# Hybrid decoder layer on one core: rope queries behind each latent tile, gate tiles beside the sums of x, and paced row loads in the down projection

## Chip, cores and metric

One core of a Trainium2 chip runs the whole layer as one program. The metric is device microseconds (us) of an execution. Matrix products run on TensorE (PE in the profile), everything elementwise on VectorE (DVE), ScalarE (ACT) and GpSimd (POOL); DMAs are issued from the queues of SyncE (SP), ACT and POOL.

## The reference, cut to what matters

```python
proj = h @ w_in[i]                      # 1024 x 1024 times 1024 x 5792
qkv, z, b_raw, a_raw, cq, ckv, kr, gate_dn, gate_mla = jnp.split(proj, SPLIT_IDX, axis=-1)
beta = jax.nn.sigmoid(b_raw)
g = -jnp.exp(dn_a_log[i]) * jax.nn.softplus(a_raw + dn_dt_bias[i])     # decays of the gated DeltaNet
...
c_q = rms_norm(cq, q_norm_w[i])                                        # query latent, 384 wide
q_nope, q_rope = jnp.split(jnp.einsum('bsc,chd->bshd', c_q, w_uq[i]), [MLA_NOPE], axis=-1)
q_rope = apply_rope(q_rope, cos, sin)                                  # 8 heads x 64
c_kv = rms_norm(ckv, kv_norm_w[i]); k_rope = apply_rope(kr, cos, sin)  # key latent, 256 wide
...
h = layer_norm(ALPHA * h + mixed @ w_o[i], ln1_g[i], ln1_b[i])
gt, up = jnp.split(h @ w_ffn_in[i], 2, axis=-1)
ffn = (jax.nn.silu(gt) * up) @ w_ffn_out[i]                            # down projection, 2816 x 1024
```

The sequence has 1024 tokens, in 8 tiles of 128. Everything is float32.

## The kernel before

Every float32 operand of a product is split into two parts, `hi` (a cast on ACT, L63) and `lo` (the remainder, on DVE, L64), and a product is three matmuls: hi·hi, hi·lo and lo·hi. A planner inside the language orders the instructions of each engine: it takes what is ready by its own timing model, earlier lines first, so work that is written later can run earlier. On the chip each engine then runs its list in that order.

**The first stage** (L129 to L397) makes everything of `proj` that is not in pairs:
- L182 to L206: the first three of the 24 *gate tiles* (`z` and the two gates; 48 matmuls each on two of the PSUM banks A to D), while x arrives. The third one's weights lie in memory of `cqT`.
- L265 to L289: the *latent tiles*. For `ckv` (336 columns with the key rope and the decays' inputs) and then for `cq` (384 columns), each of 8 token tiles takes 24 matmuls into a PSUM tile `s`, a sum of squares on ACT, a scale on DVE and POOL, the product with the norm weight on DVE (L285), 2 or 3 transposes on PE (L288) and a split into `ckvT` or `cqT`. The weights `wA` have 8 buffers, so those of `cq` follow when the last tile of `ckv` gives them back.
- L302 to L351: rope of the keys and the decays (some 35 small operations on DVE and ACT).
- L353 to L395: gate tiles 3 to 6 (L164 to L176), and for each token tile the *rope queries*: 9 matmuls (L379), six DVE operations (L294 to L299), a split, 8 transposes (L393), two copies on ACT (L394) into `qt` (two buffers), and a store to `qr_d` issued from POOL (L395). The latents are spilled to DRAM (`lat_d`) in six large stores from POOL.
- L420 to L440: the sums of x (`T1` to `T4`) that the seven-product scheme of the next stage needs, with their splits. Gate tile 7 is written between them (L435). Then `pair` (L458, products at L480) runs, whose matmuls may not start before the last rope transpose (L616).

**The last stage** (L1357 to L1498) is the down projection in seven products (n = 1, 2, 7, 5, 6, 3, 4), each of 11 steps (k) with 12 matmuls per step (L1433). A step loads an activation form (`x_form`, L1372: two `xs` buffers with a split into three `xh` buffers for n = 1 and 2; straight into `xh`, 2 x 256 KB, for n = 3, 5, 6, 7) and takes a weight form (`w_form`, L1387) from rows of `w_ffn_out`, four quarters of 11 rows of 256 KB. Quarter (0, 0) is loaded in `open_down`; `load_rows` brings the others ahead of the product that first uses them:

```python
        if n == 2:
            load_rows((0, 1))
        elif n == 7:
            load_rows((1, 0))
        elif n == 5:
            load_rows((1, 1))
```

The planner is free to issue all of these loads, all on SP's queue, as soon as their memory is free.

Of the kernel before, what the change touches and what calls it, by code (L numbers as in the profile page):

```python
# [17 lines left out]
P = 128  # L18
# [18 lines left out]
def tile_hybrid_block(ctx: ExitStack, tc: tile.TileContext, A: dict):  # L37
# [143 lines left out]
    pp = pool(p1, "p1")  # L181
    p1w = ExitStack()  # L182
    pw1 = pool(p1w, "p1w")
    fw = [[[half_w(i) for i in range(2)] for _ in range(2)] for _ in range(2)]
    fps = [[bank(0), bank(1)], [bank(2), bank(3)], [s_tile(), s_tile()]]
    for k in range(KT):
# [7 lines left out]
        if k == 0:  # L194
            fv = [cqT[i][:, 0].rearrange("p (k a) -> p k a", k=KT) for i in range(2)]
            fw.append([[v[:, q * 4:q * 4 + 4] for v in fv] for q in range(2)])
# [68 lines left out]
    for off, wd, c0, n, dst in ((0, 336, CQ, 2, ckvT), (336, 384, 0, 3, cqT)):  # L265
        if off:
            wA = lat_w(off, wd)
        nl_ = n * P
        for t in range(NT):
            ts = slice(t * P, (t + 1) * P)  # L270
            ps = s_tile()
            for k in range(KT):
                for j, (a, b) in enumerate(HL):
                    nc.tensor.matmul(ps[:, 0:wd], xT[a][k][t // 4][:, t % 4 * P:(t % 4 + 1) * P], wA[k][b][:, 0:wd], start=(k == 0 and j == 0),
                                     stop=(k == KT - 1 and j == 2))
            if off == 0:
                nc.scalar.copy(kr_raw[:, t], ps[:, 256:320])
                nc.scalar.copy(ba[:, t], ps[:, 320:336])
            mr = pp.tile([P, 2], F32, name="mr", bufs=3)
            ms, rs = mr[:, 0:1], mr[:, 1:2]  # L280
            cn = pw1.tile([P, CQ], F32, name="cn", bufs=3)[:, 0:nl_]
            nc.scalar.activation(cn, ps[:, 0:nl_], AF.Square, accum_out=ms)
            nc.vector.tensor_scalar(ms, ms, 1.0 / nl_, 1e-6, op0=ALU.mult, op1=ALU.add)
            nc.gpsimd.tensor_tensor(rs, ms, nhalf[:, 0:1], ALU.pow)
            nc.vector.scalar_tensor_tensor(cn, ps[:, 0:nl_], rs, wn[:, c0:c0 + nl_], op0=ALU.mult, op1=ALU.mult)  # L285
            tp = s_tile("t")[:, 0:nl_].rearrange("p (n a) -> p n a", n=n)
            for j in range(n):
                nc.tensor.transpose(tp[:, j], cn[:, j * P:(j + 1) * P], ident)  # L288
            split(tp, dst[0][:, :, ts], dst[1][:, :, ts])  # L289

    p1w.close()
# [9 lines left out]
    kr2 = pp.tile([P, NT, 2, RD], F32, name="kr2")  # L301
    rtmp = pp.tile([P, NT, 32], F32, name="rtmp")  # L302
    rope(kr2[:, :, 0, 0:32], kr2[:, :, 0, 32:64], kr_raw[:, :, 0:32], kr_raw[:, :, 32:64], cos, sin, rtmp)
    nc.vector.tensor_copy(kr2[:, :, 1], kr2[:, :, 0])
    for hf in range(2):
        tp = s_tile("t").rearrange("p (t a) -> p t a", t=4)
        for t in range(4):
            nc.tensor.transpose(tp[:, t], kr2[:, hf * 4 + t].rearrange("p a b -> p (a b)"), ident)
        split(tp, *[k.rearrange("p (t a) -> p t a", t=NT)[:, hf * 4:hf * 4 + 4] for k in krT])

    for i in range(2):
        nc.gpsimd.dma_start(out=lat_d["ckv"][i], in_=ckvT[i])

    e1 = pp.tile([P, NT, H], F32, name="e1")
    nc.scalar.activation(e1, ba[:, :, 0:8], AF.Exp, scale=-1.0)
    nc.vector.tensor_scalar(e1, e1, 1.0, None, op0=ALU.add)
    nc.vector.reciprocal(beta, e1)
    xa = pp.tile([P, NT, H], F32, name="xa")
    nc.vector.tensor_tensor(xa, ba[:, :, 8:16], alog[:, 1].unsqueeze(1).broadcast_to([P, NT, H]), ALU.add)
    na = pp.tile([P, NT, H], F32, name="na")  # L320
    nc.vector.scalar_tensor_tensor(na, xa, -1.0, xa, op0=ALU.mult, op1=ALU.min)
    y = pp.tile([P, NT, H], F32, name="y")
    nc.scalar.activation(y, na, AF.Exp)
    den = pp.tile([P, NT, H], F32, name="den")
    nc.vector.tensor_scalar(den, y, 2.0, None, op0=ALU.add)
    nc.vector.reciprocal(den, den)
    sa = pp.tile([P, NT, H], F32, name="sa")
    nc.vector.tensor_tensor(sa, y, den, ALU.mult)
    s2 = pp.tile([P, NT, H], F32, name="s2")
    nc.vector.tensor_tensor(s2, sa, sa, ALU.mult)  # L330
    acc = pp.tile([P, NT, H], F32, name="acc")
    nc.vector.tensor_scalar(acc, s2, 2.0 / 17, 2.0 / 15, op0=ALU.mult, op1=ALU.add)
    for n in (13, 11, 9, 7, 5, 3, 1):
        nc.vector.tensor_tensor(acc, acc, s2, ALU.mult)
        nc.vector.tensor_scalar(acc, acc, 2.0 / n, None, op0=ALU.add)
    nc.vector.tensor_tensor(acc, acc, sa, ALU.mult)
    nc.vector.scalar_tensor_tensor(acc, xa, 0.0, acc, op0=ALU.max, op1=ALU.add)
    nea = row[:, 24:32]
    nc.scalar.activation(nea, alog[:, 0], AF.Exp)
    g = pp.tile([P, NT, H], F32, name="g")  # L340
    nc.vector.scalar_tensor_tensor(g, acc, -1.0, nea.unsqueeze(1).broadcast_to([P, NT, H]), op0=ALU.mult, op1=ALU.mult)
    split(g, g_hl[:, 0], g_hl[:, 1])
    gc = s_tile()[:, 0:P].rearrange("p (a t h) -> p a t h", a=2, t=NT)
    nc.tensor.matmul(gc[:, 0], m_le, g, start=True, stop=True)
    nc.tensor.matmul(gc[:, 1], ones, g, start=True, stop=True)
    nc.scalar.activation(eg, gc[:, 0], AF.Exp)
    nc.scalar.activation(egl, gc[:, 1], AF.Exp)
    gcs = pp.tile([P, NT, H], F32, name="gcs")
    nc.vector.tensor_copy(gcs, gc[:, 0])
    nc.vector.tensor_tensor(gcs, gc[:, 1], gcs, ALU.subtract)  # L350
    nc.scalar.activation(egd, gcs, AF.Exp)  # L351

    gate_tile(3)  # L353
    gate_tile(4)
    w5 = load_w(A["w_main"][24 + 5])


    pb_s = ExitStack()
    pb = pool(pb_s, "p1b")
    wq = [pb.tile([P, 3, 512], F32R, name=f"wq{i}") for i in range(2)]  # L360
    for k in range(3):
        st = wpool.tile([P, 512], F32, name="wst", bufs=2)
        nc.sync.dma_start(out=st, in_=A["w_uq_rope"][:, k])
        split(st, wq[0][:, k], wq[1][:, k])
    SPILL = {2: [("kr", krT, 0), ("kr", krT, 1)], 3: [("cq", cqT, 0)], 4: [("cq", cqT, 1)]}
    for t in range(NT):
        if t == 0:
            gate_tile(5, w5)
        if t == 3:
            gate_tile(6)  # L370
        for nm, v, i in SPILL.get(t, ()):
            nc.gpsimd.dma_start(out=lat_d[nm][i], in_=v[i].unsqueeze(1) if nm == "kr" else v[i])
        with tc.high_priority():
            ts = slice(t * P, (t + 1) * P)
            ps = s_tile()
            n = 0
            for k in range(3):
                for a, b in ((0, 0), (0, 1), (1, 0)):
                    nc.tensor.matmul(ps, cqT[a][:, k, ts], wq[b][:, k], start=n == 0, stop=n == 8)  # L379
                    n += 1  # L380
            pv = ps.rearrange("p (h r) -> p h r", h=H)
            qro = pb.tile([P, H, RD], F32, name="qro", bufs=2)
            qtmp = pb.tile([P, H, 32], F32, name="qtmp", bufs=1)
            cb = trigq[:, 0, t].unsqueeze(1).broadcast_to([P, H, 32])
            sb = trigq[:, 1, t].unsqueeze(1).broadcast_to([P, H, 32])
            rope(qro[:, :, 0:32], qro[:, :, 32:64], pv[:, :, 0:32], pv[:, :, 32:64], cb, sb, qtmp)
            stk = pb.tile([P, H, 2, RD], F32R, name="stk", bufs=2)
            split(qro, stk[:, :, 0], stk[:, :, 1])
            qt = pb.tile([P, H, P], F32R, name="qt", bufs=2)
            for hf in range(2):  # L390
                tp = s_tile("t").rearrange("p (h a) -> p h a", h=4)
                for h in range(4):
                    p1b_end = nc.tensor.transpose(tp[:, h], stk[:, hf * 4 + h].bitcast(F32).rearrange("p a b -> p (a b)"), ident)  # L393
                nc.scalar.copy(qt[:, hf * 4:hf * 4 + 4], tp)  # L394
            nc.gpsimd.dma_start(out=qr_d[:, :, ts].rearrange("h p n -> p h n"), in_=qt)  # L395
# [1170 lines left out]
```

## Time and profile before

| | us |
|---|---|
| median of 3 runs | 2138.59 (2135.35 to 2140.73) |
| the profiled execution's own time | 2146.9 |
| its span | 2145.1 |
| PE busy | 2051.5 (96%) |
| DVE / ACT / POOL busy | 1388.8 / 945.8 / 651.2 |
| mean granted clock of TensorE | 0.982 of full |

The busy share of PE counts a matmul as busy for longer when the granted clock is lower. So a stretch has to be read by its number of matmuls and its granted clock, not by its busy share alone. A row of the views by stretch gives, for each engine, the busy us and the number of instructions, then the clock, the busy share of the DMA engines and GB/s.

### The profile page before, as it was taken

The page shows a single profiled execution, that of the slowest core. Times are in us where ns is not written, and L with a number is a line of the kernel's source. Part 1 is how long each engine was busy: PE and PEld are TensorE (multiplying, and loading weights), DVE is VectorE, ACT ScalarE, POOL GpSimd, SP SyncE. Part 2 cuts the span into 40 slices and gives each one's busy share as a digit, 9 for nine tenths or more (in the row PEclk, how much of TensorE's full clock was granted, in tenths as well). Part 3 has the DMA queues.
Part 4 walks back from the last instruction along what each step waited for, and adds up shares of the span by engine and source line. Part 5 has one row for each costly group of instructions (what it writes and reads, how often), then busy time and mean ns, then how long its engine had stood idle before and what let it go on. Part 6 is the DMA issues. An engine that isn't in the chain of part 4 may idle for free.

```text
span 2145.1 us, 29573 instructions
## 1 busy us (share of the span) xinstructions
PE 2051.5 (96%) x10450; PEld 1718.9 (80%) x10450; DVE 1388.8 (65%) x2151; ACT 945.8 (44%) x1936; POOL 651.2 (30%) x569
## 2 busy tenths in 40 slices
PE   8998899999999999998999999999999999998998
PEld 6987578787878888786887788899888888886876
DVE  4434988797955655443645356487878788864476
ACT  5333556776675555444433223243333333333233
POOL 0112443444342899840210000100111121111842
PEclk9999999999999999998999999999999999999999
DMA  6236345556566321137986666025434344376562
GB/s 221 73 131 169 103 171 185 172 186 212 198 212 248 102 75 59 58 109 211 293 246 208 209 221 237 22 87 178 148 112 144 128 143 134 114 246 246 192 230 108
DMA packets 225892, 350.86 MB, mean 164 GB/s; under 512 B 43792, under 2 KB 118352, under 8 KB 224464
## 3 DMA queue, kind: packets, MB, share of 16 engines
q1 hardware_dynamic: 208400, 318.67, 44.8%
q0 software_dynamic: 12736, 22.02, 3.5%
q10 hardware_dynamic: 4608, 8.27, 1.1%
q8 instruction: 83, 1.36, 0.3%
q14 instruction: 65, 0.53, 0.1%
HBM read 228.01 MB, written 120.88 MB: 163 GB/s over the span
## 4 chain that ended last, share of the span: by engine, by line
PE 62%; DMA 11%; DVE 7%; ACT 6%; issue 2%; POOL 1%; SPq 0%; POOLq 0%; ACTq 0%; DVEq 0%
PE f L1433 6%; PE A L1242 5%; PE s L1199 4%; PE f L1115 4%; PE f L717 4%; PE B L1242 3%; PE D L1242 3%; PE E L1242 3%; PE C L1242 3%; PE F L1242 3%; PE o L741 2%; PE C L480 2%; PE D L480 2%; PE B L480 2%; PE p L689 2%
## 5 line engine op out<-in xcount | busy, mean ns | idle before, releaser
L1433 PE MATMUL f<-wh,xh 128*128 128x512 f32 x792 | 186.6, 395 | 10.7 <-ACT xh L63 9.0
L1433 PEld LDWEIGHTS f<-wh,xh 128*128 128x128 f32 x792 | 150.0, 190 | 46.5 <-ACT xh L63 11.1
L63 ACT CAST w<-S 128x512 fp32r<-128x512 f32 x168 | 103.5, 618 | 137.0 <-PE D L1242 42.9
L1341 POOL TENSOR_TENSOR T<-act 128x512 f32<-128x512 f32 x22 | 32.2, 1463 | 402.0 <-DVE act L1326 231.0
L64 DVE TENSOR_TENSOR w<-S,w 128x512 fp32r<-128x512 f32 x168 | 131.5, 783 | 25.5 <-ACT w L63 21.2
L1242 PE MATMUL A<-m,w 128*128 128x512 f32 x504 | 121.2, 389 | 0.0
L876 PE MATMUL y<-om,w 128*128 128x512 f32 x384 | 103.5, 414 | 8.5 <-ACT w L63 3.5
L1242 PEld LDWEIGHTS A<-m,w 128*128 128x128 f32 x504 | 94.5, 188 | 19.6
L805 POOL TENSOR_TENSOR nl<-nl,itmp 128x486 f32<-128x486 f32 (+44 forms) x106 | 105.5, 1012 | 1.4
L803 POOL TENSOR_TENSOR itmp<-nl 128x486 f32<-128x486 f32 (+44 forms) x106 | 95.0, 914 | 17.3 <-DMA nl<-n_d 12.8
L1088 POOL TENSOR_TENSOR lrs<-sm,nhalf 128x1 f32<-128x1 f32 x16 | 23.2, 1455 | 234.9 <-issue 140.1
L876 PEld LDWEIGHTS y<-om,w 128*128 128x128 f32 x384 | 71.5, 195 | 26.5 <-ACT om L63 4.7
L64 DVE TENSOR_TENSOR w<-wst,w 128x512 fp32r<-128x512 f32 (+1 forms) x54 | 51.7, 957 | 61.8 <-ACT w L63 61.8
L1115 PE MATMUL f<-wo,m 128*128 128x512 f32 x384 | 91.0, 392 | 0.6 <-DVE acc L1079 0.6
L1115 PEld LDWEIGHTS f<-wo,m 128*128 128x128 f32 x384 | 71.4, 188 | 15.5 <-DVE acc L1079 1.1
L63 ACT CAST w<-wst 128x512 fp32r<-128x512 f32 (+1 forms) x54 | 43.3, 808 | 91.8 <-DMA wst<-in_w_br_mla_dram 39.9
L64 DVE TENSOR_TENSOR pt<-t,pt 128x512 fp32r<-128x512 f32 (+1 forms) x96 | 52.2, 554 | 46.5 <-ACT pt L63 45.6
L741 PE MATMUL o<-pt,vv 128*128 128x512 f32 (+3 forms) x288 | 78.2, 374 | 3.5 <-ACT pt L63 1.4
L528 DVE SCALAR_TENSOR_TENSOR c<-zo,cw,c 128x1023 f32<-128x1023 f32 (+2 forms) x48 | 70.4, 1467 | 14.0 <-ACT c L526 13.8
L721 DVE TENSOR_REDUCE row<-f 128x1 f32<-128x128 f32 (+3 forms) x64 | 48.3, 755 | 42.1 <-PE f L719 41.5
L717 PE MATMUL f<-c,qn 128*128 128x512 f32 (+3 forms) x288 | 68.9, 357 | 1.8 <-ACT pr L723 1.8
L1199 PE MATMUL s<-r,m 128*128 128x256 f32 x576 | 69.7, 283 | 0.0
(479 smaller groups left out, 5388.1 us busy)
## 6 DMA issues: line engine op xcount, KB each, us to landing
acc<-in_w_ffn_in_dram SPq DMA_DIRECT2D x44, 512.0 KB, 4.0
xs_d<-xo SPq DMA_DIRECT2D x88, 256.0 KB, 2.5
xh<-xs_d SPq DMA_DIRECT2D x88, 256.0 KB, 2.8
wst<-in_w_main_dram SPq DMA_DIRECT2D x25, 512.0 KB, 4.7
a<-in_w_ffn_out_dram SPq DMA_DIRECT2D x44, 256.0 KB, 5.2
raw<-in_w_main_dram SPq DMA_DIRECT2D x20, 512.0 KB, 4.4
xs<-xf_d SPq DMA_DIRECT2D x33, 256.0 KB, 3.4
an_d<-c SPq DMA_DIRECT2D x16, 512.0 KB, 6.9
```

The source lines that it names most:

```text
L63: nc.scalar.copy(hi, src)
L64: nc.vector.tensor_tensor(lo, src, hi.bitcast(F32), ALU.subtract)
L480: nc.tensor.matmul(bk, w[a][:, k], x[b][k], start=(k == 0 and j == 0), stop=(k == 3 and j == 2))
L717: nc.tensor.matmul(ps[:, c * 512:c * 512 + w], l[:, qs], r[c][:, 0:w], start=n == 0, stop=(n == 4 and c != gq))
L741: nc.tensor.matmul(po[:, i0 * P:512], vv[kt][a][:, hh * P:(hh + 1) * P], hl[b][:, 0:w], start=(kt == 0 and j == 0), stop=(kt == last and j ...
L803: nc.gpsimd.tensor_tensor(tv, nl[:, k0:kn_, k:k + 1].broadcast_to([P, kn_ - k0, w]), nl[:, k:k + 1, k + 1:64].broadcast_to([P, kn_ - k0, w ...
L805: nc.gpsimd.tensor_tensor(nl[:, k0:kn_, k + 1:64], nl[:, k0:kn_, k + 1:64], tv, ALU.subtract)
L876: nc.tensor.matmul(ps, w[a][:, k], od[b][:, k, ns] if dn else om[k][b], start=(k == 0 and j == 0), stop=(k == KT - 1 and j == 2))
L1115: nc.tensor.matmul(ps[:, ns], mT[a][kh, t // 4][:, k % 4, t % 4 * P:(t % 4 + 1) * P], wo[k][b][:, ns], start=(k == 0 and j == 0), stop=(k ...
L1199: nc.tensor.matmul(ps, mT[a][k // 4, t // 4][:, k % 4, tq], wg[k][b], start=(k == 0 and j == 0), stop=(k == KT - 1 and j == 2))
L1242: nc.tensor.matmul(bank, w[a][:, k], x[b][:, k], start=(k == 0 and j == 0), stop=(k == 3 and j == 2))
L1433: nc.tensor.matmul(bk, x[a][:, t * P:(t + 1) * P], w[b], start=(k == 0 and j == 0), stop=(k == HH - 1 and j == 2))
```

## The change

It does four things.
1. The rope queries of tile t are written right behind the latent tile t of `cq` and take it from a two-buffer tile, on banks A to D; their weights are loaded and split ahead. `cqT`, `ckvT` and `krT` are gone: each latent piece is stored to DRAM at once, two stores per tile, issued from ACT. The `qr_d` store moves from POOL to SP.
2. The rope of the keys and the decays become a generator, `side`, of which one piece follows each rope tile.
3. Gate tiles 3 to 7 are written beside the sums of x: tile 3 ahead of the loop, one more in each of its four turns.
4. In the down projection one row is loaded per step, one product earlier than before, and each row and each load of `acc` is issued on SP only behind the newest activation load.

```diff
+    def latent(t, off, wd, c0, n, wA):
...
+        out = [latp.tile([P, n, P], F32R, name=f"l{n}{i}", bufs=2) for i in range(2)]
+        split(tp, *out)
+        for i in range(2):
+            nc.scalar.dma_start(out=lat_d["ckv" if off == 0 else "cq"][i][:, :, ts], in_=out[i].bitcast(F32))
+        return out
+
+    for t in range(NT):
+        latent(t, 0, 336, CQ, 2, wA)
+    wA = lat_w(336, 384)
+    wq = [wq_tile(i) for i in range(2)]
+    for k in range(3):
+        st = wpool.tile([P, 512], F32, name="wst", bufs=2)
+        nc.sync.dma_start(out=st, in_=A["w_uq_rope"][:, k])
+        split(st, wq[0][:, k], wq[1][:, k])
...
-    gate_tile(3)
-    gate_tile(4)
-    w5 = load_w(A["w_main"][24 + 5])
...
+    def rope_q(t, cq):
+        ts = slice(t * P, (t + 1) * P)
+        ps = bank(t % 2)
...
+                nc.tensor.matmul(ps, cq[a][:, k], wq[b][:, k], start=n == 0, stop=n == 8)
...
+            tp = bank(2 + hf).rearrange("p (h a) -> p h a", h=4)
...
+            nc.scalar.copy(qt[:, hf * 4:hf * 4 + 4], tp)
+        nc.sync.dma_start(out=qr_d[:, :, ts].rearrange("h p n -> p h n"), in_=qt.bitcast(F32))
+        return end
+
+    steps = side()
     for t in range(NT):
-        if t == 0:
-            gate_tile(5, w5)
-        if t == 3:
-            gate_tile(6)
...
+        p1b_end = rope_q(t, latent(t, 336, 384, 0, 3, wA))
+        next(steps, None)
+    for _ in steps:
+        pass
...
+    gate_tile(3)
     for k in range(4):
+        gate_tile(4 + k)
         st = []
...
-    gate_tile(7)
...
-                nc.sync.dma_start(out=hl[i].bitcast(F32), in_=xs_d[n][k][i])
+                came[0] = nc.sync.dma_start(out=hl[i].bitcast(F32), in_=xs_d[n][k][i])
...
-        if n == 2:
-            load_rows((0, 1))
-        elif n == 7:
-            load_rows((1, 0))
-        elif n == 5:
-            load_rows((1, 1))
+        q = {1: (0, 1), 2: (1, 0), 7: (1, 1)}.get(n)
+        if q:
+            wr[q] = []
+        if n == 5:
             ln2 = ln_consts("ln2_g", "ln2_b")
...
-            for t, cs in need.get((n, k), ()):
...
+            with tc.issue_after(came[0].ins):
+                if q:
+                    load_row(q, k)
+                for t, cs in need.get((n, k), ()):
+                    if t == len(acc):
+                        acc.append(acc_tile())
+                    nc.sync.dma_start(out=acc[t][:, cs], in_=acc_d[t][:, cs])
```

## Rows read from the trace of the kernel before

**Rows 1.** The page: busy time of each engine, share of the span, instructions.

```profile
PE 2051.5 (96%) x10450; PEld 1718.9 (80%) x10450; DVE 1388.8 (65%) x2151; ACT 945.8 (44%) x1936; POOL 651.2 (30%) x569
```

**Rows 2.** Busy time by stretch, first stage and first pairs.

```profile
94.00:150.00 56.00, 56.00 (x305) 51.49 (x304) 17.52 (x49) 14.07 (x36) 8.00 (x14) 1.00 0.33 122
150.00:164.00 14.00, 10.41 (x32) 7.25 (x31) 8.29 (x20) 6.40 (x10) 0.00 (x0) 0.76 0.66 228
164.00:198.50 34.50, 34.50 (x178) 28.51 (x177) 20.01 (x44) 12.84 (x23) 10.14 (x9) 1.00 0.57 150
198.50:213.00 14.50, 8.47 (x38) 6.99 (x37) 2.07 (x3) 4.84 (x10) 2.57 (x3) 0.76 0.97 259
213.00:244.00 31.00, 21.31 (x68) 13.38 (x67) 28.50 (x30) 15.16 (x31) 17.37 (x12) 0.83 0.36 102
```

**Rows 3.** Timeline of PE: start, us, work [idle before it <- who ended it].

```profile
197.96 0.48 PE L170 MATMUL D<-xT,w 128*128 128x512 f32 x1
...
205.56 1.97 PE L393 MATMUL t<-masks,stk 128*128 128x128 f32 x8 [5.16 <-ACT qt L394]
...
220.55 1.95 PE L480 MATMUL A<-T,w 128*128 128x512 f32 x3 [4.17 <-ACT T L63]
...
263.38 2.88 PE L480 MATMUL C<-xT,w 128*128 128x512 f32 x12
266.10 2.89 PE L480 MATMUL D<-T,w 128*128 128x512 f32 x12
```

**Rows 4.** Timeline of ACT beside the last rope queries.

```profile
204.92 0.59 ACT L394 CAST qt<-t 128x512 fp32r<-128x512 f32 x1 [4.73 <-DMA qr_d<-qt]
```

**Rows 5.** Groups of DVE in 213 to 244 us: busy us, mean ns | idle before.

```profile
L64 DVE TENSOR_TENSOR T<-e,T 128x512 fp32r<-128x512 f32 x12 | 12.1, 1041 | 0.7 <-ACT T L63 0.7
```

**Rows 6.** Timeline of PE: a `ckv` run, a `cq` run, one tile's rope queries.

```profile
58.98 5.16 PE L274 MATMUL s<-wA,xT 128*128 128x336 f32 x32
...
104.37 6.68 PE L274 MATMUL s<-wA,xT 128*128 128x384 f32 x37
...
170.40 2.21 PE L379 MATMUL s<-wq,cqT 128*128 128x512 f32 x9
```

**Rows 7.** Timeline of all engines behind one latent tile of `cq`.

```profile
111.14 0.49 ACT L282 ACTIVATE cn<-s 128x384 f32<-128x384 f32 x1 [3.58 <-PE s L274]
...
112.64 0.62 DVE L285 SCALAR_TENSOR_TENSOR cn<-s,mr,wn 128x384 f32<-128x384 f32 x1 [0.73 <-POOL mr L284]
113.26 0.48 ACT L63 CAST cqT<-t 128x384 fp32r<-128x384 f32 x1 [1.54 <-PE t L288]
113.78 0.56 DVE L64 TENSOR_TENSOR cqT<-t,cqT 128x384 fp32r<-128x384 f32 x1 [0.51 <-ACT cqT L63]
```

**Rows 8.** Timeline of DVE: first and last of six rope operations.

```profile
177.20 0.42 DVE L294 TENSOR_TENSOR qro<-s,trigq 128x256 f32<-128x256 f32 x1 [1.14 <-PE s L379]
...
179.11 0.42 DVE L299 TENSOR_TENSOR qro<-qro,qtmp 128x256 f32<-128x256 f32 x1
```

**Rows 9.** Timeline of SP: last five loads of the second `wA`.

```profile
81.96 6.43 SPq L213 DMA_DIRECT2D wst<-in_w_lat_dram  x5
```

**Rows 10.** Timeline of ACT: its cast of the eighth, and one DMA issue.

```profile
90.39 0.51 ACT L63 CAST wA<-wst 128x384 fp32r<-128x384 f32 x1 [1.13 <-DMA wst<-in_w_lat_dram]
...
183.87 0.33 ACTq L176 DMA_DIRECT2D z_d<-zo  x1
```

**Rows 11.** Busy time by stretch, down projection.

```profile
1930.00:1960.00 30.00, 21.03 (x75) 15.42 (x74) 13.17 (x18) 10.73 (x19) 5.54 (x4) 0.89 0.91 339
1940.00:1950.00 10.00, 7.51 (x24) 5.48 (x24) 5.26 (x7) 3.08 (x6) 3.62 (x3) 0.83 1.05 406
1978.00:2008.00 30.00, 30.00 (x134) 24.85 (x133) 15.03 (x16) 6.84 (x11) 25.68 (x18) 1.00 0.60 194
```

**Rows 12.** Chain that ended last, 1860 to 2145 us: start, us, link.

```profile
1924.72 7.34 DMA a<-in_w_ffn_out_dram
...
1947.64 5.10 DMA xs<-xf_d
```

More of the change, by code (lines that the diff above doesn't have):

```diff
@@ L264, in tile_hybrid_block @@
     ba = pp.tile([P, NT, 16], F32, name="ba")
-    for off, wd, c0, n, dst in ((0, 336, CQ, 2, ckvT), (336, 384, 0, 3, cqT)):
-        if off:
-            wA = lat_w(off, wd)
+    def latent(t, off, wd, c0, n, wA):
         nl_ = n * P
[L269 to L289, printed above, removed]
@@ L291, in tile_hybrid_block @@
-    p1w.close()
+        ts = slice(t * P, (t + 1) * P)
+        ps = s_tile("s" if t or off else "t")
+        for k in range(KT):
+            for j, (a, b) in enumerate(HL):
+                nc.tensor.matmul(ps[:, 0:wd], xT[a][k][t // 4][:, t % 4 * P:(t % 4 + 1) * P], wA[k][b][:, 0:wd], start=(k == 0 and j == 0),
+                                 stop=(k == KT - 1 and j == 2))
+        if off == 0:
+            nc.scalar.copy(kr_raw[:, t], ps[:, 256:320])
+            nc.scalar.copy(ba[:, t], ps[:, 320:336])
@@ new lines, in latent @@
+        for j in range(n):
+            nc.tensor.transpose(tp[:, j], cn[:, j * P:(j + 1) * P], ident)
+        out = [latp.tile([P, n, P], F32R, name=f"l{n}{i}", bufs=2) for i in range(2)]
[7 more added lines that the diff above has]
+    wq = [wq_tile(i) for i in range(2)]
@@ L299, in rope @@
         nc.vector.tensor_tensor(out2, out2, tmp, ALU.add)
[L301 to L351, printed above, removed]
@@ L353, in tile_hybrid_block @@
-    gate_tile(3)
-    gate_tile(4)
-    w5 = load_w(A["w_main"][24 + 5])
[L358 to L365, printed above, removed]
-    for t in range(NT):
-        if t == 0:
-            gate_tile(5, w5)
-        if t == 3:
-            gate_tile(6)
[L371 to L395, printed above, removed]
@@ L1356, in tile_hybrid_block @@
     fo = [None, None]
-    upper, wr, ready = {}, {}, {}
+    upper, wr, ready, came = {}, {}, {}, [None]
     lo, hi = slice(0, 512), slice(512, 1024)
@@ L1365, in load_row @@
         wr[q].append(v)
-    def load_rows(q):
-        wr[q] = []
-        for k in range(HH):
-            load_row(q, k)
     def x_form(n, k):
```

111 lines of the change are left out of this document (96 added, 15 removed).

## The prediction, made before the changed kernel was run

> **What bounds the kernel now.** I read the page's engine shares first, then the busy time by stretch in the two stages that the change touches, then the timelines and the chain of waits inside the bad stretches. PE is busy 96% of the span [rows 1], so nothing gains unless PE stops waiting or gets its clock back; the change removes no matmul. The yardstick is the start-to-start time of twelve 512-column matmuls at full clock, 266.10 - 263.38 = 2.72 us [rows 3], so 0.2267 us each.
>
> In the first stage PE runs dense at clock 1.00 from 94 to 150 us and from 164 to 198.5 us [rows 2], and poorly in three stretches. 150 to 164: 32 matmuls are worth 7.3 us, so 6.7 us are lost. 198.5 to 213: 38 instructions, 12 of them transposes; eight take 1.97 us at the low clock [rows 3], so about 0.12 each at the full one; 26 x 0.2267 + 1.5 = 7.4, lost 7.1. Here ACT stood 4.7 us for a `qr_d` store that held a `qt` buffer [rows 4], and PE 5.2 us behind ACT [rows 3]. 213 to 244: 68 matmuls are worth 15.4, lost 15.6; DVE is busy 28.5 of the 31 us [rows 2] on the sums of x and their splits [rows 5], and PE waits for them [rows 3]. **Together 29.4 us.** The granted clock there is 0.76 to 0.83, between the levels of 1.2 and 2.4 GHz, after idle time of PE.
>
> In the down projection 1930 to 1960 us holds 75 matmuls, worth 17.0, so **13.0 us are lost**. In the chain of waits the row loads of `w_ffn_out` follow one another and an activation load comes out behind them [rows 12], with the DMA engines full at 406 GB/s [rows 11]: all 33 rows (3 quarters of 11) were issued ahead of the activations of the first two products. The most that the change can give back is 42.4 us.
>
> **The change part by part.**
>
> *Gate tiles beside the sums of x.* The five tiles are 5 x 48 x 0.2267 = 54 us of PE work that needs nothing from the sums. It covers 28.5 us of DVE plus 10 weight splits of the gates at about 1 us [rows 5]. So the 15.6 us go, and T4's splits, which now wait for gate tile 7, lie beside products that need no sum. If the planner runs gates early, the cover shrinks; even then 6 us is the most I would leave in the forecast's case. I take 0.
>
> *Rope queries behind each latent.* 150 to 164 and 198.5 to 213 disappear as they are (13.8 us), for the stores no longer share the time of the x loads, but PE loses its filler in the latent stage. Three places can open.
> (a) Within a stage: a `ckv` tile is 24 matmuls, 24 x 5.16/32 = 3.9 us, a `cq` tile 24 x 6.68/37 = 4.3 us [rows 6]. From the end of its matmuls to the end of the DVE product that frees `s` is 111.14 to 113.26, 2.1 us [rows 7]. With two `s` buffers that is shorter than the next tile's matmuls, so PE stays dense; the rope matmuls (2.2 us) and transposes add work, not waiting. Cost 0.
> (b) At the change of `wA`: the five last weight loads take 6.43 us to issue [rows 9] and the eighth is cast at 90.39 [rows 10], about 1.2 us per weight tile. One latent tile needs 3 x 0.18 = 0.54 us of PE per weight tile, two need 1.08. Over eight that leaves 1 to 5.3 us open that gates filled before, and up to 3.1 us more if the clock falls (150 to 164 lost 6.7 us with 3.6 us idle, 14.00 - 10.41 [rows 2]). I take 4, nearer to the upper end since the last `ckv` tile still holds one `s`.
> (c) At the end: behind the last `cq` tile come 2.1 to the product, 0.5 for transposes, 1.1 for the split [rows 7], 2.2 rope matmuls [rows 6], 2.3 rope on DVE [rows 8], 1.1 split, 1.2 transposes: 10.5 us, in which PE has 3.9 us of that chain itself and 3.4 us of tile 6 if that is late. Open: 3.2 to 6.6 us, with a clock loss at most 9.7; 0 if a gate fills it on a bank that is already free. I take 5.
>
> *Queues.* The latents make 36 small stores issued from ACT at 0.33 us [rows 10], 12 us over some 100 us in which ACT is busy a quarter to a half [rows 2]; each waits for DVE's half of its split, and the next square on ACT queues behind it, for which (a) has 2 us to spare. Without that cover it would be 12 us. POOL loses its stores; SP gets eight `qr_d` stores, behind which only gate weights and x loads queue, needed 11 us or more later. The small decay operations move but stay the same: hidden under PE, as in 94 to 150. Casting DRAM tiles to another type costs nothing.
>
> *Paced rows.* The row of step k is put behind the newest activation load on SP and is used a product later, so the first two products carry 512 KB per 2.72 us, 193 GB/s, against 406. The 13.0 us go. The added order has its price in product n = 7: 22 activation loads, 11 rows and 8 loads of `acc`, 41 x 0.262 = 10.7 MB. At 406 GB/s that is 26.5 us; at the rate of 1978 to 2008 when busy, 194/0.60 = 323 [rows 11], it is 33.3, against 132 x 0.2267 = 29.9 of PE. So 0 to 3.4 us come back; I take 1.5. A short burst of rows when their memory comes free costs 0 to 2, I take 1: an activation behind them is several steps ahead.
>
> **Sum.** First stage 29.4 - 4 - 5 = 20.4; down projection 13.0 - 2.5 = 10.5; together 30.9. The profiled execution took 2146.9 us and would become 2116.0. It lies 8.3 us (0.4%) above the median of the runs, 2138.59; against that I predict 2107.7, say 2108.
>
> The granted clock deserves one check. The stretch 164 to 198.5 us mixes rope transposes and matmuls at 1.00 [rows 2], and the new rope stage has 11 transposes beside 33 matmuls per tile. The Trainium skill (TensorE: Matmul & The Clock Gate, Part 4: PE-mode transpose) says that transposes do not count as PE activity for the clock as matmuls do. By that rule the end of the rope work, where transposes are nearly alone, runs slow, as 198.5 to 213 did; it is the rule behind the last rival.
>
> **Rivals.**
> - *The gaps move instead of closing.* Terms (b), (c) and the cover at their upper ends, 8.4 + 9.7 + 6 = 24.1, and the down projection keeps 5.4: the gain is 42.4 - 29.5 = 12.9, time 2126. For it: the filler is gone. Against: the two-buffer arithmetic of (a).
> - *The written place of the gates does nothing.* Gate tile 7 is written among the sums of x, yet it ran ahead of the last rope transposes: its matmul at 197.96 stands before the one row of eight at 205.56 [rows 3]. If the planner draws all five forward again, (b) and (c) are filled, but the sums stay bare: 42.4 - 15.6 - 5 = 22, time 2117.
> - *Rows still bunch.* The order binds a row to the issue of an activation load, not its arrival; if activations are issued far ahead, the rows follow. Against: two `xs` and three `xh` buffers, so at most five rows, 1.3 MB, 3 us at 406. Otherwise only the first stage gains: 2118.
> - *Slower: PE takes latent and rope in written order.* In each of 8 tiles PE would then idle for 2.1 + 1.1 + 2.3 + 1.1 = 6.6 us, 53 us in all, and the clock would add up to 3.1 us per tile. 53 - 42 = 11 over now, 36 with the clock: about 2160. It decides from 42.4/8 = 5.3 us of idle time per tile. Against: before, the planner put other tiles' matmuls between a tile's product and its transposes, with PE dense [rows 2].
> - *The rope stage loses its clock.* 8 x (4.3 + 2.2 + 1.4) = 63 us at half the rate adds 63, less 42: 2160. Against: the clock of 1.00 in 164 to 198.5.
>
> **How the numbers follow.** 0.3% is 6.4 us, about what a measurement of this kernel can tell from no change. Chances: forecast 0.62; gaps move 0.12; gates drawn forward 0.10; rows bunch 0.04; PE in written order 0.06; clock lost 0.02; and 0.04 that the new plan costs so much in stages which the change does not touch that nothing is left. The first four are faster, but 0.03 of the gaps that move could end within 0.3%: faster 0.85, same 0.03 + 0.04 = 0.07, slower 0.08. The range runs from the whole 42.4 us, 2096, to the gaps' case, 2126, plus 2 us for the spread of the runs: 2096 to 2128. It takes in the second and third rival.
>
> **What would show it.** Right: from the sums of x on, L170 matmuls of PE beside DVE's `T` splits at clock 1.00; no wait of ACT on `qr_d`; at most two short PE gaps, at the second `wA` and at the last rope tile; 1930 to 1960 us worth of down projection with about 132 matmuls at 1.00 and DMA below 0.8; n = 7 with DMA near full. Wrong: L170 again between 94 and 150 us with PE waiting for `T`; idle time of PE before every L379 or L393; or the chain still led by `w_ffn_out` loads.

## The result, and the profile after

The changed kernel takes 2113.55 us (median of 4 runs, 2113.03 to 2117.28); the kernel before, run beside it, 2138.45 us (4 runs, 2135.35 to 2140.73). The ratio is 0.9883, with a 95% interval of 0.9867 to 0.9898: 24.9 us faster, outside the 0.3% that a measurement can tell from no change. The forecast was 2108.0 in a range of 2096 to 2128. The profiled execution of after took 2113.03 us, its span is 2111.2 us.

The page of after, busy time of each engine, which answers to [rows 1]:

```profile
PE 2035.8 (96%) x10450; PEld 1713.7 (81%) x10450; DVE 1386.4 (66%) x2151; ACT 945.6 (45%) x1935; POOL 640.5 (30%) x555
```

As many matmuls as before, and the same share. The share says nothing of the gain, because the span shrank with it. Where the time came from is read from landmarks in the two timelines of PE. First before, the last products of the pairs and the first row of the down projection (start, us, matmuls):

```profile
684.15 2.88 PE L480 MATMUL D<-xT,w 128*128 128x512 f32 x12
...
1908.35 6.96 PE L1433 MATMUL f<-wh,xh 128*128 128x512 f32 x30
```

Then after, the same:

```profile
666.13 2.88 PE L490 MATMUL D<-xT,w 128*128 128x512 f32 x12
...
1881.30 21.92 PE L1439 MATMUL f<-wh,xh 128*128 128x512 f32 x96
```

The pairs end 18.0 us earlier: their last twelve matmuls start at 684.15 before and at 666.13 after, and end 2.88 us later. The down projection began at 1908.35 and lasted to the end of the span, 236.8 us; now it begins at 1881.3 and lasts 229.9 us, 6.9 less. Together 24.9, which is the gain of the medians. Between the two landmarks lie the stages that the change does not touch: 1221.3 us before (687.03 to 1908.35), 1212.3 after. These 9 us are the excess of the one profiled execution of before (2146.9 against its median of 2138.45); the first experiment tests that.

**The first stage after**, busy time by stretch (us, busy us and instructions of PE, PEld, DVE, ACT, POOL, then clock, DMA share, GB/s), against [rows 2]:

```profile
75.00:90.00 15.00, 12.03 (x68) 10.79 (x68) 12.48 (x43) 6.72 (x19) 1.65 (x3) 0.99 0.41 119
90.00:110.00 20.00, 20.00 (x108) 19.02 (x108) 10.21 (x29) 4.96 (x12) 1.10 (x2) 0.92 0.27 83
110.00:160.00 50.00, 48.68 (x269) 42.46 (x268) 24.63 (x61) 18.16 (x40) 2.28 (x4) 1.00 0.52 159
160.00:190.00 30.00, 24.85 (x99) 20.00 (x98) 21.34 (x23) 15.46 (x30) 12.68 (x8) 0.89 0.59 207
190.00:244.00 54.00, 54.00 (x240) 44.69 (x240) 29.49 (x38) 20.18 (x34) 16.19 (x11) 1.00 0.29 98
```

Latents with rope queries (110 to 160) run nearly dense at full clock, and 190 to 244, where PE used to wait for the sums of x, holds 240 matmuls: 54 / 0.2267 = 238, all that fits. Two holes are left. At the change of `wA` 2.97 us are idle (75 to 90) and the clock of 0.92 behind it costs 20 x 0.08 = 1.6: 4.6 us. Of the 2.97 only 0.93 are waits for the weights (0.78 and 0.15); 2.02 stand behind the first two `cq` tiles. Their matmuls ran interleaved and ended together (ACT squared them at 87.15 and 87.63), so both `s` buffers were full until DVE had the first product ready at 89.28. From 160 to 190, 99 matmuls are worth 22.4 us: 7.6 lost. The timeline of PE shows both, the rope transposes between the gates, and the first pair:

```profile
79.58 1.07 PE L272 MATMUL s<-wA,xT 128*128 128x384 f32 x3 [0.78 <-DVE wA L64]
80.81 0.80 PE L272 MATMUL s<-wA,xT 128*128 128x384 f32 x3 [0.15 <-DVE wA L64]
...
89.43 0.57 PE L286 MATMUL t<-masks,cn 128*128 128x128 f32 x3 [2.02 <-DVE acc L350]
...
144.09 5.73 PE L166 MATMUL A<-xT,w 128*128 128x512 f32 x24
149.67 0.60 PE L394 MATMUL C<-masks,stk 128*128 128x128 f32 x4
...
173.11 8.26 PE L166 MATMUL C<-xT,w 128*128 128x512 f32 x24 [5.15 <-ACT zo L171]
...
208.41 2.88 PE L490 MATMUL A<-xT,w 128*128 128x512 f32 x12
```

From 144 us on the gate tile on the free banks A and B fills the waits of the last rope query. Then comes gate tile 3 on C and D, and the next one waits 5.15 us until ACT has emptied C. What ACT did instead, from its timeline:

```profile
164.66 0.62 ACT L63 CAST T<-e 128x512 fp32r<-128x512 f32 x1 [7.18 <-DVE e L440]
165.19 0.61 ACT L63 CAST w<-wst 128x512 fp32r<-128x512 f32 x1
167.19 1.21 ACT L63 CAST T<-e 128x512 fp32r<-128x512 f32 x2 [1.39 <-POOL e L442]
170.01 0.62 ACT L63 CAST T<-e 128x512 fp32r<-128x512 f32 x1 [1.61 <-DVE e L440]
170.53 0.61 ACT L63 CAST w<-wst 128x512 fp32r<-128x512 f32 x1
171.16 1.28 ACT L171 ACT_TABLE_LOAD   x1
172.46 0.60 ACT L171 ACTIVATE zo<-C 128x512 f32<-128x512 f32 x1
```

In ACT's list the casts of the sums (`T`) stand ahead of the gates' activations (`zo`), so ACT waited for sums, 7.18 us in one place, while the finished banks A and B stood full. The sums were late since their loads were: DVE's first sum waited 5.73 us for one, until 163.93. SP's timeline:

```profile
145.60 11.63 SPq L396 DMA_DIRECT2D qr_d<-qt  x3
158.23 0.34 SPq L150 DMA_DIRECT2D wst<-in_w_main_dram  x1
158.64 14.01 SPq L435 DMA_DIRECT2D c<-in_xT_dram  x7
```

The loads of x left SP at 158.64, behind the last `qr_d` stores and a weight load.

**The down projection after**, busy time by stretch, against [rows 11]:

```profile
1890.00:1910.00 20.00, 15.04 (x63) 12.10 (x62) 7.03 (x12) 6.92 (x12) 0.00 (x0) 0.89 0.90 305
1910.00:1930.00 20.00, 20.00 (x84) 16.43 (x83) 11.54 (x17) 9.30 (x18) 2.59 (x2) 0.94 0.60 199
1950.00:1970.00 20.00, 19.88 (x88) 16.16 (x87) 8.33 (x7) 3.73 (x6) 20.00 (x15) 1.00 1.00 368
```

40 / 0.2267 = 176.4 matmuls fit from 1890 to 1930, and 147 ran: 6.7 us lost, where before lost 13.0. In product n = 7 (1950 to 1970) the DMA engines are full at 368 GB/s and PE is idle for 0.12 us. The hole, in the timelines of SP, ACT and PE:

```profile
1893.15 0.32 SPq L1385 DMA_DIRECT2D xs<-xf_d  x1
...
1894.09 7.37 SPq L1374 DMA_DIRECT2D a<-in_w_ffn_out_dram  x8
1901.56 0.38 SPq L1385 DMA_DIRECT2D xs<-xf_d  x1
...
1907.51 0.62 ACT L63 CAST xh<-xs 128x512 fp32r<-128x512 f32 x1 [3.64 <-DMA xs<-xf_d]
...
1908.18 22.01 PE L1439 MATMUL f<-wh,xh 128*128 128x512 f32 x87 [4.96 <-ACT xh L63]
```

Eight rows left in one burst, 7.37 us of SP's queue (some 3.8 of them waits of SP for earlier transfers, by its own list of waits). The next activation load left behind them at 1901.56, was cast 5.95 us later, and PE stood for 4.96 us.

### The profile page after: what moved, and what is told of

It reads as the page before. It is cut to its first block, busy times and chain, and to the rows that moved or that the text cites. A ratio compares the mean times of both kernels' runs of the same rounds, so it can differ in the third digit from the quotient of the medians.

```text
span 2111.2 us, 29647 instructions
## 1 busy us (share of the span) xinstructions
PE 2035.8 (96%) x10450; PEld 1713.7 (81%) x10450; DVE 1386.4 (66%) x2151; ACT 945.6 (45%) x1935; POOL 640.5 (30%) x555
## 4 chain that ended last, share of the span: by engine, by line
PE 70%; DMA 10%; ACT 7%; DVE 7%; issue 3%; POOL 1%; SPq 0%; ACTq 0%; POOLq 0%; DVEq 0%
PE f L1439 6%; PE A L1252 5%; PE f L1125 4%; PE f L727 4%; PE s L1209 4%; PE F L1252 3%; PE D L1252 3%; PE E L1252 3%; PE C L1252 3%; PE B L1252 3%; PE C L490 3%; PE s L272 2%; PE B L490 2%; PE o L751 2%; PE A L490 2%
## 5 line engine op out<-in xcount | busy, mean ns | idle before, releaser
L813 POOL TENSOR_TENSOR itmp<-nl 128x486 f32<-128x486 f32 (+44 forms) x106 | 93.3, 898 | 16.8 <-DMA nl<-n_d 12.3
L1125 PEld LDWEIGHTS f<-wo,m 128*128 128x128 f32 x384 | 71.4, 188 | 15.6 <-DVE acc L1089 1.1
L538 DVE SCALAR_TENSOR_TENSOR c<-zo,cw,c 128x1023 f32<-128x1023 f32 (+2 forms) x48 | 70.6, 1471 | 13.2 <-ACT c L536 13.0
```

The costliest lines, as they stand in the source:

```text
L813: nc.gpsimd.tensor_tensor(tv, nl[:, k0:kn_, k:k + 1].broadcast_to([P, kn_ - k0, w]), nl[:, k:k + 1, k + 1:64].broadcast_to([P, kn_ - k0, w ...
L1125: nc.tensor.matmul(ps[:, ns], mT[a][kh, t // 4][:, k % 4, t % 4 * P:(t % 4 + 1) * P], wo[k][b][:, ns], start=(k == 0 and j == 0), stop=(k ...
```

## The experiments

Gains in single stages are read from profiles (end of the pairs, start and length of the down projection), since the stages between scatter. Times of versions are compared with the kernel before of the same job.

**1. The kernel before once more, unedited** (b_again).

> The kernel before, unchanged, profiled once more. In the two profiles the change gains 18 us up to the last matmul of the pairs, another 9 us in the scan and output branches (first product of that stage at 1000.6 us before and 980.0 after, its last at 1267.8 and 1240.3), and 6.9 us in the down projection; together 33.9, while the runs say 24.9. Theory: the 9 us belong to the one profiled execution of before (2146.9 us against a median of 2138.45), not to the change; then this profile takes about 2138 us and the stage from 1000 to 1268 us is 6 to 9 us shorter than it was, as after the change. Rival: the change itself speeds that stage up, by its different spills; then this profile shows the same stage as long as before.

Measured: 2137.85 us. Its pairs end at 688.5 and its down projection begins at 1900.8, so the stages between take 1212.3 us, as in after. One stretch of them, in the first profile of before and then in this one:

```profile
970.00:1000.00 30.00, 25.82 (x158) 20.23 (x157) 8.00 (x17) 11.02 (x25) 0.00 (x0) 0.77 0.79 224
```

```profile
970.00:1000.00 30.00, 24.69 (x192) 20.14 (x190) 9.44 (x20) 13.43 (x31) 0.00 (x0) 1.00 0.83 238
```

The same program ran 34 PE instructions more in 30 us, at a granted clock of 1.00 in place of 0.77. So the 9 us are the execution's and not the change's.

**2. and 3. Each half alone.** first_only has the changed first stage with the old down projection, down_only the reverse. Their edits are the diff ahead of the prediction, cut at the down projection; in first_only that is:

```diff
-        q = {1: (0, 1), 2: (1, 0), 7: (1, 1)}.get(n)
-        if q:
-            wr[q] = []
-        if n == 5:
+        if n == 2:
+            load_rows((0, 1))
+        elif n == 7:
+            load_rows((1, 0))
+        elif n == 5:
+            load_rows((1, 1))
             ln2 = ln_consts("ln2_g", "ln2_b")
...
-            with tc.issue_after(came[0].ins):
-                if q:
-                    load_row(q, k)
```

> The first stage of the changed kernel with the down projection of before. Theory: the two halves add up, and the first stage is worth 18 us: 2120 us (2117 to 2123). Rival (the scan stage gains as well): 2112 us or less. Rival (the halves only shift waits to each other): 2125 us or more.

> The kernel before with the down projection of the changed one. Theory: 6.9 us faster, 2131.5 us (2129 to 2134), with one idle time of PE of about 5 us left in the first product, behind a burst of row loads. Rival, from the prediction's own term: 10.5 us, 2128 us, if the gap that is left depends on the first stage.

Measured, beside 2140.93 us for the kernel before: first_only 2124.18 us, ratio 0.9923 (0.9894 to 0.9951), 16.8 us; down_only 2133.15 us, ratio 0.9956 (0.9939 to 0.9972), 7.8 us. The sum, 24.5, is within half a microsecond of the 24.9 of the whole change. So close a sum is partly chance, for the intervals are some 12 and 7 us wide, and first_only missed its 2117 to 2123 (beside a kernel before that ran 2.5 us longer than in the job of the result). The profiles show the same without them: the pairs of first_only end at 670.0 and its down projection lasts 236.0 us, as before; for down_only it is 687.0 and 228.3, with the burst of eight rows and an idle time of 3.97 us behind it. The halves add up, and no sign is seen that one hands time to the other.

**4. The gate tiles beside the sums, without the new order of latents and rope queries** (gates_late).

```diff
-    gate_tile(3)
-    gate_tile(4)
-    w5 = load_w(A["w_main"][24 + 5])
...
-        if t == 0:
-            gate_tile(5, w5)
-        if t == 3:
-            gate_tile(6)
...
+    gate_tile(3)
     for k in range(4):
+        gate_tile(4 + k)
...
-    gate_tile(7)
```

> The kernel before with one part of the change alone: gate tiles 3 to 7 are written beside the sums of x, and the latents, the ropes, the spills and the down projection stay as they were. Theory that the cover of the sums is what gains: the 15.6 us lost from 213 to 244 us go, the rope queries lose their filler and cost some of it, 8 to 15 us faster in all (2123 to 2130). Rival that the rope queries must first be moved behind the latents: with rope alone on PE the gaps there grow by as much as the sums give back, 2135 to 2142 us.

Measured: 2133.6 us, ratio 0.9962 (0.9944 to 0.998), 7.3 us; the pairs end at 680.6. Between the two expectations, and the stretches say why:

```profile
90.00:140.00 50.00, 37.82 (x198) 34.77 (x197) 17.55 (x44) 11.52 (x31) 5.47 (x10) 0.84 0.30 111
140.00:200.00 60.00, 60.00 (x295) 49.56 (x294) 25.57 (x56) 22.55 (x39) 8.24 (x9) 0.99 0.68 170
200.00:220.00 20.00, 19.09 (x85) 15.48 (x83) 18.96 (x18) 9.14 (x16) 14.29 (x10) 1.00 0.62 203
220.00:240.00 20.00, 16.54 (x60) 13.22 (x61) 17.40 (x22) 16.14 (x35) 8.83 (x6) 0.83 0.22 78
```

The sums are covered (200 to 220 at clock 1.00), but the old order of latents and rope queries, bare of its gates, leaves PE idle for 12 of the 50 us from 90 to 140, 7.90 of them in one wait for the rope weights. In PE's and ACT's timelines:

```profile
132.80 2.93 PE L372 MATMUL s<-wq,cqT 128*128 128x512 f32 x6 [7.90 <-ACT wq L63]
```

```profile
132.13 0.62 ACT L63 CAST wq<-wst 128x512 fp32r<-128x512 f32 x1 [8.90 <-DMA wst<-in_w_uq_rope_dram]
```

So the gates alone gain less than half of what the whole first stage gains. Not all of the rest needs the rope queries behind the latents: the changed kernel also loads and splits the rope weights ahead, and gates_late with that part alone was not tried. The hole behind ACT is here too:

```profile
223.46 5.49 PE L474 MATMUL C<-xT,w 128*128 128x512 f32 x12 [4.37 <-ACT zo L175]
```

**5. Each row four steps later** (rows_shift), to see whether the burst is what holds the down projection.

```diff
-        q = {1: (0, 1), 2: (1, 0), 7: (1, 1)}.get(n)
-        if q:
-            wr[q] = []
...
-                if q:
-                    load_row(q, k)
+                step = i * HH + k - 4
+                if 0 <= step < 3 * HH:
+                    q = ((0, 1), (1, 0), (1, 1))[step // HH]
+                    wr.setdefault(q, [])
+                    load_row(q, step % HH)
```

> The changed kernel (median 2113.55 us), but in the down projection each row is bound to the activation load four steps later, and the three quarters follow one another without a break. In the profile of the changed kernel eight rows are issued together at 1894 to 1901 us, when their memory comes free, and PE then stands idle for 5.0 us and runs at the lower clock: 6.7 us lost in 1890 to 1930. Theory that the burst is the cause: four rows instead of eight, the idle time shrinks below 1.5 us, 5 us faster than the changed kernel: 2107 to 2110 us. Rival that the activations come late by themselves (their stores of the last pairs): no gain, 2112 to 2115 us, with the idle time still there.

Measured, beside 2143.68 us for the kernel before: 2107.21 us, ratio 0.9828 (0.9813 to 0.9842). Stretches, then SP's burst:

```profile
1890.00:1910.00 20.00, 19.19 (x84) 15.23 (x83) 8.89 (x14) 7.73 (x14) 0.00 (x0) 1.00 0.92 315
1910.00:1930.00 20.00, 19.35 (x85) 15.42 (x84) 14.05 (x19) 10.45 (x19) 3.10 (x2) 1.00 0.61 201
```

```profile
1895.48 4.66 SPq L1374 DMA_DIRECT2D a<-in_w_ffn_out_dram  x4
```

Four rows leave together in place of eight, the clock stays at 1.00, 169 matmuls run in the 40 us (1.7 us lost, not 6.7), and the down projection lasts 224.3 us, 5.6 less. Over all profiles it lasts 227.7 to 229.9 us with the rows as in after (six), and 222.2 to 224.7 with the rows four steps later (four). The DMA engines are as busy as in after from 1890 to 1910 (0.92 against 0.90), and the stores of the last pairs are where they were. So the burst was the cause, and not the activations by themselves. What in it counts more is not separated: the activation leaves SP behind the rows, and the loads of activations also land later, after a median of 5.8 us in 1890 to 1910 of after against 3.3 in 1910 to 1950. Its size is explained too: in after as here, eight activation loads had left SP ahead of the burst, and the rows bound to them left together, eight there and, with four steps' distance, four here.

**6. to 8. Three ways to the hole of 5.15 us at the sums of x.** x_pool issues the loads of x from POOL, zo_first puts ACT's casts of the sums behind the gates' activations, gate3_early writes gate tile 3 ahead of the second set of latent weights.

```diff
-            nc.sync.dma_start(out=v, in_=A["xT"][:, r * 4 + k])
+            nc.gpsimd.dma_start(out=v, in_=A["xT"][:, r * 4 + k])
```

```diff
-    gate_tile(3)
+    g3 = gate_tile(3)
...
-        gate_tile(4 + k)
+        gk = gate_tile(4 + k)
...
-            split(v, *[xq[nm][i][k] for i in range(2)])
+            with tc.issue_after((gk if k == 0 else g3).ins):
+                split(v, *[xq[nm][i][k] for i in range(2)])
```

```diff
         latent(t, 0, 336, CQ, 2, wA)
+    gate_tile(3)
     wA = lat_w(336, 384)
...
-    gate_tile(3)
     for k in range(4):
         gate_tile(4 + k)
```

> The changed kernel, but the eight loads of x for the sums are issued from POOL instead of SP. In the profile of the changed kernel the first of them leaves SP at 158.6 us, right behind the last store of rotated queries and a gate weight load that waits for a split, and PE later stands idle for 5.2 us (167.8 to 173.1) and runs at the lower clock: 7.5 us lost from 160 to 180. Theory that SP's order makes the sums late: the loads start several us earlier, 3 to 6 us faster: 2107.5 to 2110.5. Rival that their memory comes free only with the last rope tile: the loads start at 157 us or later on POOL as well, 2112 to 2115 us.

> The changed kernel, but on ACT the casts of the first sums are put behind the activations of gate tile 4, and those of the other sums behind the activations of gate tile 3. In the profile of the changed kernel bank C waits for its activation until 172.5 us, because ACT has the casts of the sums ahead of it. Theory that the order on ACT makes the hole, whatever the x loads do: the idle time of 5.2 us falls below 2.5, 4 to 6 us faster: 2107.5 to 2109.5. Rival: the sums end later by as much and PE waits for them at the first pairs: 2112 to 2115 us.

> The changed kernel, but gate tile 3 is written ahead of the second set of latent weights, so that it can fill PE there. The changed kernel idles 0.9 us for these weights and 2.0 us behind the first two latent tiles of cq, and the clock falls after it: about 4 us lost from 75 to 110. Theory that the missing filler is the cause: 2 to 4 us faster: 2109.5 to 2111.5. Rival: the planner uses the tile up before (between latent tiles that need no filler) and the cover of the sums is 11 us shorter: 2112 to 2118 us.

Measured, beside the same 2143.68 us: x_pool 2109.72 us (ratio 0.9827, 0.9805 to 0.985), zo_first 2109.34 (0.9838, 0.9822 to 0.9854), gate3_early 2109.24 (0.9839, 0.9824 to 0.9854). The three times do not tell them apart, and the changed kernel was not in this job; the profiles tell more. The hole in x_pool, with its stretch:

```profile
170.86 7.39 PE L166 MATMUL C<-xT,w 128*128 128x512 f32 x24 [3.12 <-ACT zo L171]
```

```profile
160.00:190.00 30.00, 26.88 (x112) 21.73 (x111) 22.35 (x24) 16.29 (x32) 13.93 (x11) 0.94 0.48 171
```

Its first loads of x on POOL, and ACT beside them:

```profile
134.20 1.82 POOL L435 DMA_DIRECT2D c<-in_xT_dram  x3 [1.72 <-ACT egd L371]
```

```profile
147.45 0.59 ACT L395 CAST qt<-C 128x512 fp32r<-128x512 f32 x1 [5.50 <-DMA qr_d<-qt]
```

The same in zo_first:

```profile
168.53 5.73 PE L166 MATMUL C<-xT,w 128*128 128x512 f32 x24 [2.17 <-ACT zo L171]
```

```profile
160.00:190.00 30.00, 27.83 (x124) 22.71 (x123) 22.51 (x24) 16.29 (x32) 13.46 (x8) 1.00 0.60 212
```

And the stretches of gate3_early:

```profile
75.00:90.00 15.00, 15.00 (x88) 14.01 (x87) 8.03 (x23) 7.64 (x22) 3.24 (x3) 1.00 0.36 101
90.00:110.00 20.00, 16.72 (x93) 15.26 (x92) 13.25 (x45) 7.80 (x18) 1.62 (x3) 1.00 0.32 107
160.00:190.00 30.00, 30.00 (x138) 24.91 (x137) 17.21 (x18) 10.25 (x18) 10.09 (x6) 1.00 0.70 232
```

In x_pool the first three loads leave from 134.20, 24 us earlier, so the rival, that their memory comes free only at 157, is out. They shorten the hole to 3.12 us, but the clock still falls behind it (0.94), and the pairs end only 0.6 us earlier (668.4); its time within the expected range says nothing then. Part of its gain was lost again, since ACT now waited 5.50 us for a `qr_d` store. ACT's order shortens the hole to 2.17 us, the clock holds at 1.00, and the pairs end at 664.4, 4.6 earlier; PE does not wait for the sums at the first pairs (240 matmuls from 190 to 244, as in after). Gate tile 3 written early removes the hole at the sums (138 matmuls instead of 99 from 160 to 190) and fills 75 to 90 (88 PE instructions instead of 68). The wait behind the first two `cq` tiles stays, in 90 to 110 and at full clock, with 2.96 us in place of 2.02; the pairs end at 659.5, 9.5 earlier. So of the 5.15 us ACT's order took 2.98 away and earlier loads 2.03; the two parts may overlap, and no version has both edits.

**9. to 12. The versions put together**, beside the changed kernel itself, on one chip, in five rounds. combo_g3 has the edits of rows_shift and gate3_early, combo_zo those of rows_shift and zo_first, combo_all adds the edit of x_pool to combo_g3; after_again is after unedited.

> The changed kernel once more, unedited, as the measure for the three versions beside it. In one job three versions of it took 2107 to 2110 us beside a kernel before that ran some 5 us longer than in the job of the changed kernel itself. Theory: what those versions gained was real, and the changed kernel comes out at 2111 to 2118 us again. Rival: the difference was between jobs, and it comes out below 2110.

> Two edits together: each row of the down projection's weights four steps later, and gate tile 3 written ahead of the second set of latent weights. Theory: the burst of rows and the holes of the first stage are separate terms, as the two halves of the change were. Rows four steps later give 5 to 6 us (6.7 us were lost in the stretch with the burst, 1.4 us of idle time stayed); gate tile 3 as filler at the change of weights gives up to 9.5 us at the last pair matmul, of which 1 to 4 stayed at the end in its own run. Together 6 to 10 us under the changed kernel in the same job, the down stage at 224 to 225 us, its start at 1880 plus or minus 2. Rival: what the first stage gains is lost again behind it, and only the rows count: 5 us.

> Two edits together: each row four steps later, and the ACT casts of the sums of x behind the activations of the gate tile beside them. Theory: PE's last hole at the sums of x came from ACT's order; alone the edit kept the clock at 1.00 and shortened the hole from 5.15 to 2.17 us. Together with the rows 8 to 10 us under the changed kernel in the same job. Rival: the gates' activations were not what counted, and only the rows do: 5 us.

> Three edits together: rows four steps later, gate tile 3 ahead of the second latent weights, and the loads of x for the sums issued from POOL in place of SP. Theory: the loads of x from POOL only shorten the hole at the sums, which gate tile 3 written early has removed already, so the third edit adds nothing: within 2 us of the version with the first two. Rival: earlier loads of x also bring the first pairs forward, and it is 2 to 4 us faster still.

| | median, us | range | ratio to before (2141.9) | interval |
|---|---|---|---|---|
| after_again | 2117.01 | 2114.35 to 2121.03 | 0.9886 | 0.9865 to 0.9907 |
| combo_g3 | 2103.09 | 2099.36 to 2104.24 | 0.9817 | 0.9802 to 0.9833 |
| combo_zo | 2103.11 | 2096.49 to 2105.18 | 0.9815 | 0.9794 to 0.9836 |
| combo_all | 2102.84 | 2101.11 to 2104.49 | 0.9819 | 0.9804 to 0.9834 |

The changed kernel repeats its ratio (0.9886 against 0.9883), with the same hole in the down projection: 142 matmuls where 176.4 fit, and again a burst of eight rows. The stretch, then SP's row:

```profile
1890.00:1930.00 40.00, 34.92 (x142) 28.28 (x141) 19.44 (x30) 16.72 (x30) 4.31 (x4) 0.91 0.79 267
```

```profile
1900.06 8.01 SPq L1374 DMA_DIRECT2D a<-in_w_ffn_out_dram  x8
```

All three combinations are 14 us faster than the changed kernel and beat both kernels. For combo_g3 the profiles give the parts: pairs 669.0 to 660.0, 9.0 us; down projection 228.8 to 224.6, 4.2 us; together 13.2 of the measured 13.9. That is over the 6 to 10 expected, because the expectation took the first stage's gain to be lost again behind it, as gate3_early alone seemed to show (its stages between took 1220.2 us); after_again, which has none of the edits, took 1218.4 there, so that loss was scatter. For combo_zo, of which 8 to 10 were expected, it is 7.8 and 6.6 us. The third edit in combo_all adds nothing (0.25 us), as the theory had it. Which of the two ways to the hole is better the medians do not tell: they agree to 0.02 us, within ranges of 5 to 9 us. Both of them together were not tried. Across jobs even the ratios are not that fine: rows_shift alone had 0.9828 and x_pool alone 0.9827, within the intervals of the combinations, though their own stages gained 5.6 and 0.6 us.

## Why the prediction was right, and where it was off

The direction and the range held, the range easily: it was 32 us wide and took in two of the rivals. The forecast was 5.5 us too low. Against the median of before it took 30.9 us and got 24.9; the 6.0 too much split into 3.6 in the down projection and 2.4 in the first stage.

- *The yardstick and the ceiling.* Counting matmuls against 0.2267 us, and not reading the busy share, gave 29.4 + 13.0 us. 18.0 and 6.9 came back. The 6.9 is from one pair of profiles: four with the old down projection took 235.3 to 237.8 us and six with the new one 227.7 to 229.9, 8.0 less by their means, so that term's miss is 2.5 to 3.6 us. No term outside the two stages was needed (experiments 1 to 3).
- *"A short burst of rows when their memory comes free costs 0 to 2, I take 1: an activation behind them is several steps ahead."* **This is the step that failed.** It cost 6.7 us. The bound behind it ("at most five rows, 1.3 MB, 3 us at 406") counted the buffers of activations and stopped there. But a row's place on the queue is behind an activation load's *issue*, and ahead of the rows SP's list has as many activation loads as the planner chose to put there, of which the first were used up by then. Eight had left, so eight rows followed at once; by the sum of the prediction these are 2.1 MB, 5.2 us at 406. They held SP for 7.37 us, and the activation behind them was not several steps ahead: it was the next one that PE needed. Four steps' distance took 5.6 us of it away (experiment 5; 4.2 and 6.6 in combo_g3 and combo_zo). The rival of the bunching rows was right in its mechanism, and its condition, five rows at most, was wrong.
- *Product n = 7: 0 to 3.4, I take 1.5.* It measured 0.12 us of idle time in 20 us. The DMA engines were full as foreseen, but at 368 GB/s, not at the 323 that the row of another stretch gave [rows 11], and at 368 the 10.7 MB need 29.1 us against 29.9 of PE.
- *(a) latents dense, 0.* Right but for the first two `cq` tiles, see (b): 1.3 us idle in the 50 from 110 to 160, at clock 1.00. With it falls the slower rival of PE in written order, which needed 5.3 us of idle time per tile.
- *(b) change of `wA`, 4.* Right in size, 4.6 us, but in part by luck. The wait for weights, which it put at 1 to 5.3, was 0.93. 2.02 were the chain from a tile's matmuls to its product, which (a) had put at nothing because of the two `s` buffers: two tiles that end together fill both. The clock's 1.6 is not fixed either: in combo_zo the same wait of 2.02 us left it at 1.00.
- *(c) end of the rope queries, 5; cover of the sums, 0.* The two together measured 7.6 us against 5, and the reason was another. The end was filled, by the way that the text allowed for ("0 if a gate fills it on a bank that is already free"): banks A and B from 144.09. The cover of the sums, put at nothing with 6 as its upper end, opened because it was worked out for PE and DVE alone. The gates need ACT to empty their banks, and ACT takes its list in order: casts that waited for late loads of x stood ahead of those activations (experiments 6 to 8). "6 us is the most I would leave in the forecast's case" was 1.6 short. The step on queues had its share: x loads behind the `qr_d` stores were to be "needed 11 us or more later", and issuing the first of them 24 us earlier took 2.03 us off the hole. A step that follows ACT's list and SP's list as well would have had these waits in it.
- *Gates drawn forward.* The planner did draw one forward, which filled (c), but not all five, and 190 to 244 is dense. That rival's 15.6 us stayed gained.
- *The clock.* Stretches with transposes between other matmuls stayed at 1.00: 110 to 160 holds eight of them behind each rope tile. The Trainium skill (TensorE: Matmul & The Clock Gate, Part 4: PE-mode transpose) has transposes not counting as PE activity in the same way; no stretch of after has them nearly alone, so the rule stays untested, and the rival that went by it did not happen. Where the clock did fall in after, 90 to 110 and 160 to 190, PE had been idle before it.

## What to carry to other kernels

Order by issue paces a queue only as long as both kinds of transfers can flow: where the paced ones come late, they pile up and leave at once, so count the leading transfers that are issued by then, not the buffers, and give the paced ones a distance. Work that is to cover a wait needs every engine it passes through, so follow it to the end, to the engine that empties its PSUM bank, and look at what stands ahead of it in that engine's list. Where matmuls are moved away from a stage as filler, something else has to fill it; here the gates alone gained 7.3 us, and the whole first stage, with rope queries in their place, 16.8.

## What the runs showed of the hardware that was not expected

- **The same program scatters by 9 us in stages that nothing touched.** From the end of the pairs to the down projection, 14 profiles took 1211 to 1221 us, over all versions, and the unedited kernel before 1221.3 and 1212.3. In one stretch its granted clock was 0.77 and 1.00. 19 runs of it in one job ranged from 2135.36 to 2152.13 us. So a gain of some 5 us is told from a profile of its own stage, or from many runs; what decides the clock there stays open.
- **A hole costs more than its wait where the clock falls with it.** 5.15 us of wait before gate tiles cost 7.6 us; 2.17 us of wait in zo_first left the clock at 1.00. How long the wait is does not decide it alone: 2.02 us behind the first `cq` tiles were followed by 0.92 from 90 to 110 in after, with 108 PE instructions, and by 1.00 in combo_zo, with 119; what decides it stays open. The wait in combo_zo, and the stretch behind it:

```profile
87.66 0.52 PE L287 MATMUL t<-masks,cn 128*128 128x128 f32 x3 [2.02 <-DVE acc L351]
```

```profile
90.00:110.00 20.00, 20.00 (x119) 18.66 (x118) 9.40 (x25) 5.55 (x13) 1.10 (x2) 1.00 0.33 100
```

- **A change of ACT's function table costs 1.28 us** (171.16 in after), and it stood on the path of the hole. The Trainium skill (ScalarE: Activation LUTs, What ACT_TABLE_LOAD costs) gives 1283 ns for the load, with which the row agrees, and some 1380 ns more for a drain; the rows have the cast before it end at 171.14 and the activation begin at 172.46, so 1.32 us in all, and no such drain shows here.
